# Softmax denominators: a running sum in a seventh plane of the exponentials' tile, added by VectorE instead of GpSimd

## The chip, the core and the metric

The kernel runs as one program on one core of a Trainium2 chip. The metric is the device time of the whole program in microseconds (us), the median of several executions. Five engines work beside each other and meet through semaphores: TensorE (PE; its weight loads are listed apart as PEld), VectorE (DVE), ScalarE (ACT), GpSimd (POOL), and SyncE (SP), which issues nearly all DMAs here.

## The reference

Two layers of a transformer-like step run over 2048 latent tokens ("sample") and 256 context tokens ("prompt"). Each layer normalises and modulates its input, projects it (1024 to 2816 columns), runs three branches (attention, a short convolution, a multi-scale pooling), gates each, and projects back. The change touches only the denominators of the attention:

```
s = jnp.einsum('bqkgd,btkd->bkgqt', qblk, k).astype(jnp.float32) * scale
p = jax.nn.softmax(s, axis=-1)
return jnp.einsum('bkgqt,btkd->bqkgd', p.astype(v.dtype), v)
```

There are 8 query heads over 2 key/value heads of width 64. A latent query attends to 2048 + 256 = 2304 keys; a context query to 256.

## The kernel before, in words

Each layer is a phase A (norm, projection, branches other than attention) and a phase B (attention and output projection). Everything is float32 in value; products are made of a rounded high part and a small low part, so that TensorE runs its fast formats.

Phase B is cut into units. A unit is one head and one block of 512 latent queries: 4 blocks x 8 heads = 32 units a layer, 64 in all. A unit has nine steps (`GRP = 3` of them form a group), and each step takes 256 keys. Besides, the first block of each layer holds four prompt units of one step each. The order of the work is written out by hand: one loop over all steps issues, in every step, a fixed set of pieces to each engine. Engines run their own queues strictly in that order.

In one step:

- `qk` (lines 1163 and 1164): four matmuls give the scores `st`, 128 keys x 2 x 512 queries, in PSUM. Two such tiles exist.
- `expo` (line 1173): ScalarE writes exp of them in full float32 to `P`, then (line 1175) once more in the rounded format to `ph`. GpSimd subtracts (`padd`, line 183) to get the low part `pl`.
- `pv` (line 1209, three steps later): two matmuls with `ph`; the low parts follow at a unit's end (line 1216).
- `max_pieces` (lines 1123 and 1130, on VectorE lines 1124 and 1132): two matmuls `mx` for a unit ahead, each followed by a row maximum `mr` on VectorE. Two `mx` tiles exist, so TensorE can issue the next but one only when VectorE has read its forerunner.
- pieces of the output projection (lines 1336 to 1340) for a block that is done.

The denominators are the sums of `P` over the keys. One part of that sum is over the 128 partitions, and is a small matmul with a column of constants (`fin_b`, line 1243, tile `lc`). The other is over the key tiles, within a partition: `zsum`. For each group of three steps the tile `P` holds, in each partition, 3 x 512 x 2 numbers: step, query, and the two key tiles of a step side by side. `expo` writes with a step of two elements (`"p n t -> p t n"`), so for one query the two key tiles are neighbours in memory. `zsum` sums the six numbers of each query with one `tensor_reduce` of VectorE over two axes, cut into three pieces of 152, 190 and 170 queries, one piece in each of the next three steps (list `zq`). It writes a tile `Z`. From the second group on, GpSimd adds the previous `Z` to it (two adds a unit), and that sum is what `lc` reads after the third.

The pools: `P` has 2 buffers, `Z` 3; the tail of the last block borrows the `Z` buffers for rows of the residual (`end`, `load_x(2, ...)`). `ch` is a tile of the output projection.

Of the kernel before, what the change touches and what calls it, by code (L numbers as in the profile page):

```python
# [9 lines left out]
F32 = mybir.dt.float32  # L10
# [4 lines left out]
ALU = mybir.AluOpType  # L15
AX = mybir.AxisListType
# [80 lines left out]
def hybrid_step(ctx: ExitStack, tc: tile.TileContext, A, O):  # L97
    nc = tc.nc
# [83 lines left out]
    def padd(out, a, b, op=ALU.add):  # L182
        nc.gpsimd.tensor_tensor(out=out, in0=a, in1=b, op=op)  # L183
# [820 lines left out]
    def phase_b(l, xs_src, xp_src, xs_dst, xp_dst, nxt):  # L1004
# [3 lines left out]
        with ExitStack() as st, ExitStack() as left:  # L1008
            def pool(name, bufs=1, side="right", to=st, **kw):
                return to.enter_context(tc.tile_pool(name=name, bufs=bufs, side=side, reuse_waits="tile", **kw))  # L1010
# [50 lines left out]
            def make_unit(prompt, blk, h):  # L1061
# [11 lines left out]
                u.fh = int(PR['fh'] and blk > 0)  # L1073
                u.P, u.pp, u.low, u.z = {}, {}, [], []
                return u
# [81 lines left out]
            GRP = 3  # L1157

            def qk(u, j):
# [4 lines left out]
                    nc.tensor.matmul(out=ps[:, i, :], lhsT=u.KL[u.g][0:65, kt], rhs=u.T2, start=False, stop=True)  # L1164
                return ps

            def expo(u, j, ps):
                if u.prompt:
                    u.P[0] = wk.tile([128, 1, 512, 2], F32, tag="wo", name="Pp", bufs=4)
                elif j % GRP == 0:  # L1170
                    u.P[j // GRP] = wk.tile([128, GRP, 512, 2], F32, tag="P", name="P", bufs=2)
                P = u.P[j // GRP][:, j % GRP].rearrange("p n t -> p t n")
                nc.scalar.activation(out=P, in_=ps, func=AF.Exp, scale=0.125)  # L1173
                ph = wk.tile([128, 2, 512], F32R, tag="ph", name="ph", bufs=LAG)
                nc.scalar.activation(out=ph, in_=ps, func=AF.Exp, scale=0.125)  # L1175
                pl = wk.tile([128, 2, 512], F16, tag="pl", name="pl", bufs=LAG + 8)
                if u is units[-1]:
                    for e, c in ((padd, slice(0, PR['dc'])), (dsub, slice(PR['dc'], 512))):
                        e(pl[:, 1, c], P[:, 1, c], ph[:, 1, c], ALU.subtract)
                    padd(pl[:, 0], P[:, 0], ph[:, 0], ALU.subtract)  # L1180
                else:
                    padd(pl, P, ph, ALU.subtract)
                u.pp[j] = (ph, pl)

            def zsum(u, grp, ns):

                st = {}
                cuts = [0, PR['z1'], PR['z2'], 512] if ns == GRP else [0, 512]

                def one(i):  # L1190
                    if i == 0:
                        st["z"] = wk.tile([128, 512], F32, tag="Z", name="Z", bufs=PR['zb'])
                    z = st["z"]
                    c = slice(cuts[i], cuts[i + 1])
                    nc.vector.tensor_reduce(out=z[:, c], in_=u.P[grp][:, 0:ns, c, :].rearrange("p s n t -> p n s t"),  # L1195
                                            axis=AX.XY, op=ALU.add)
                    if i == len(cuts) - 2:
                        if grp and (u.blk or grp == 1 or not PR['zl']):
                            padd(z, z, u.z.pop())
                        u.z.append(z)  # L1200

                return [lambda i=i: one(i) for i in range(len(cuts) - 1)]

# [186 lines left out]
            def outproj_tail(B):  # L1390
# [6 lines left out]
                def load_x(t, tag, n, bufs):  # L1397
                    xs[t] = []
                    for i in range(0, D, n):
                        x = wk.tile([128, n], F32, tag=tag, name="ox", bufs=bufs)  # L1400
                        nc.sync.dma_start(out=x, in_=xs_src[rows[t], i:i + n])
                        xs[t] += [x[:, k:k + 512] for k in range(0, n, 512)]
# [30 lines left out]
                    load_w(3, 0, wk.tile([128, KD, 256], F32R, tag="P", name="wt", bufs=2), 0)  # L1433

                def end():
                    load_x(2, "Z", 512, PR['zb'])
                    load_x(3, "o", 512, 2)

                def mm(t, c, q):
# [51 lines left out]
                for t in range(4):  # L1491
                    for c in range(4):
                        rest += [lambda t=t, c=c, q=q: mm(t, c, q) for q in ((2, 0, 1, 3) if 4 * t + c >= 4 + n2 else (3,))]
                        if c % 2:
                            rest.append(lambda t=t, c=c: add(t, c // 2))
                    rest.append(lambda t=t: finish(t))
                return early, half, later, final, end, ahead, rest, beside


# [95 lines left out]
            wk = pool("b_wk")  # L1595
# [9 lines left out]
            for s in range(NSTEP + LAG + 16):  # L1605
# [50 lines left out]
                if cur:  # L1656
                    u, j = cur
                    ps = qk(u, j)
                    if ready:
                        do_pv(s)  # L1660
                    expo(u, j, ps)
                    pvq.append((u, j, s))
                    if j % GRP == GRP - 1 or j == u.nst - 1:
                        zq.extend(zsum(u, j // GRP, j % GRP + 1))
# [19 lines left out]
            slow.flush()  # L1684

    phases = [phase_b(1, xS1, xP1, xS2, xP2, None)]
    phases.append(phase_a(1, xS1, xP1, phases[-1]))
    phases.append(phase_b(0, A["x_sample"][0], A["x_prompt"][0], xS1, xP1, phases[-1]))
    phases.append(phase_a(0, A["x_sample"][0], A["x_prompt"][0], phases[-1]))
    for phase in reversed(phases):  # L1690
# [30 lines left out]
```

## Time and profile before

| what | us |
|---|---|
| median of 3 runs | 3357.68 (3351.25 to 3362.43) |
| profiled execution, its own time | 3371.42 |
| its span in the profile | 3369.6 |
| phase B of the first layer, core stretch looked at | 721 to 1600 |
| phase B of the second layer, core stretch looked at | 2385 to 3300 |

The profiled execution is 13.7 us longer than the median of the runs. Busy times are those of one execution. A busy TensorE is not a TensorE at its peak, since the ends of its matmuls are modelled; so an idle TensorE in the rows is surely idle, while a busy one may be waiting within its pipeline. "Idle before" names what ended the wait of an engine.

### The profile page before, as it was taken

Reading aid. Unit: us, or ns where it says so; the run is one execution under the profiler, and the core shown is the slowest. Engines: PE = TensorE matmul, PEld = TensorE weight load, DVE = VectorE, ACT = ScalarE, POOL = GpSimd, SP = SyncE. Lnnn points to the kernel's source line nnn. Section 1 sums busy time; section 2 is a strip of 40 time slices with the busy share of each in tenths; the row PEclk is TensorE's granted clock in tenths of the full one; section 3 lists DMA queues with packets and bytes.
Section 4 is the critical chain, followed back from the end, with each engine's and each line's share of the span. In section 5 each row is a group of like instructions: output and inputs, shape, how many; then the busy total and the mean of one; then the engine's idle time right before and its main releaser. Section 6 shows DMA issues by size and latency. Waiting matters only on the chain. (4 is left out here: it accounts for less than half of the span.)

```text
span 3369.6 us, 48369 instructions
## 1 busy us (share of the span) xinstructions
PE 3138.9 (93%) x17818; PEld 2369.1 (70%) x17818; DVE 2446.6 (73%) x3860; ACT 1845.8 (55%) x2654; POOL 2125.9 (63%) x1192
## 2 busy tenths in 40 slices
PE   6899999988999999999999999999889899998998
PEld 4788888754566666667788787887456566665667
DVE  6546474458888888888466536635898988999885
ACT  3232333248777777777433323323787677776772
POOL 3325352238998898888453435322798888887883
PEclk9999999999999999999999999999899999999999
DMA  7246645350241323133523555334113324232245
GB/s 240 79 151 197 222 131 160 128 130 23 89 144 49 97 74 97 56 114 118 203 85 117 180 181 167 113 103 114 50 54 119 123 60 128 74 111 85 76 138 197
DMA packets 377380, 402.66 MB, mean 119 GB/s; under 512 B 21940, under 2 KB 329144, under 8 KB 376632
## 3 DMA queue, kind: packets, MB, share of 16 engines
q1 hardware_dynamic: 377144, 399.56, 38.3%
q8 instruction: 142, 2.33, 0.3%
q14 instruction: 94, 0.77, 0.1%
HBM read 278.09 MB, written 121.39 MB: 119 GB/s over the span
## 5 line engine op out<-in xcount | busy, mean ns | idle before, releaser
L183 POOL TENSOR_TENSOR pl<-P,ph 128x1024 f16<-128x1024 f32 (+2 forms) x594 | 1401.4, 2379 | 242.3 <-ACT ph L1175 223.2
L1124 DVE TENSOR_REDUCE mr<-mx 128x1 f32<-128x512 f32 x1024 | 693.9, 683 | 214.5 <-PE mx L1123 210.2
L1173 ACT ACTIVATE P<-st 128x1024 f32<-128x1024 f32 x576 | 635.1, 1103 | 324.9 <-PE st L1164 313.8
L1195 DVE TENSOR_REDUCE Z<-P 128x152 f32<-128x912 f32 (+2 forms) x576 | 695.4, 1208 | 13.5 <-ACT P L1173 12.6
L1175 ACT ACTIVATE ph<-st 128x1024 fp32r<-128x1024 f32 x584 | 592.2, 1014 | 0.0
L1123 PE MATMUL mx<-KH,T 128*128 128x512 f32 x1024 | 507.7, 496 | 56.8 <-DVE mr L1124 38.1
L1163 PE MATMUL st<-T,KH 128*128 128x512 f32 x1152 | 506.0, 498 | 9.6 <-ACT ph L1175 9.6
L638 PE MATMUL rest<-xh,wh 128*128 128x512 f32 (+1 forms) x1280 | 486.1, 380 | 1.9 <-ACT wh L428 1.5
L640 PE MATMUL rest<-xh,wl 128*128 128x512 f32 (+1 forms) x1280 | 476.7, 372 | 6.7 <-DVE wl L430 4.9
L639 PE MATMUL rest<-xl,wh 128*128 128x512 f32 (+1 forms) x1280 | 476.8, 372 | 0.8 <-POOL xl L183 0.8
L1164 PE MATMUL st<-T,L 65*128 65x512 f16 x1152 | 459.4, 399 | 0.0
L1209 PE MATMUL pv<-ph,V 128*128 128x512 f32 x1152 | 385.5, 416 | 11.5 <-DVE o L1228 11.5
L1164 PEld LDWEIGHTS <-L 65*128 65x128 f16 x1152 | 113.7, 99 | 302.7 <-issue 301.8
L1123 PEld LDWEIGHTS mx<-KH,T 128*128 128x128 f32 x1024 | 200.3, 196 | 169.7 <-DVE mr L1124 104.8
L430 POOL TENSOR_TENSOR wl<-wf,wh 128x512 fp32r<-128x512 f32 x88 | 121.9, 1386 | 300.5 <-ACT wh L428 285.1
L640 PEld LDWEIGHTS rest<-xh,wl 128*128 128x128 f32 x1280 | 244.1, 191 | 50.5 <-DVE wl L430 5.9
L638 PEld LDWEIGHTS rest<-xh,wh 128*128 128x128 f32 x1280 | 244.9, 191 | 47.2 <-issue 6.3
L639 PEld LDWEIGHTS rest<-xl,wh 128*128 128x128 f32 x1280 | 244.8, 191 | 38.5 <-POOL xl L183 1.2
L477 PE MATMUL qkv<-wh,xh 128*128 128x256 f32 x864 | 252.2, 292 | 3.1 <-ACT wh L428 3.1
L478 PE MATMUL qkv<-wl,xh 128*128 128x256 f32 x864 | 248.8, 288 | 5.3 <-DVE wl L430 2.8
L1163 PEld LDWEIGHTS st<-T,KH 128*128 128x128 f32 x1152 | 229.8, 200 | 26.4 <-ACT ph L1175 12.7
L479 PE MATMUL qkv<-wh,xl 128*128 128x256 f32 x864 | 247.9, 287 | 0.0
(231 smaller groups left out, 5833.0 us busy)
## 6 DMA issues: line engine op xcount, KB each, us to landing
wo<-woH SPq DMA_DIRECT2D x68, 512.0 KB
wo<-woL SPq DMA_DIRECT2D x68, 512.0 KB
wf<-in_w_in SPq DMA_DIRECT2D x50, 512.0 KB
wa<-in_w_ada SPq DMA_DIRECT2D x24, 1024.0 KB
wf<-in_w_in SPq DMA_DIRECT2D x19, 1024.0 KB
woH<-wgh SPq DMA_DIRECT2D x64, 256.0 KB
woL<-wgl SPq DMA_DIRECT2D x64, 256.0 KB
xS<-ox SPq DMA_DIRECT2D x24, 512.0 KB
```

The lines of the kernel that those rows point to most:

```text
L183: nc.gpsimd.tensor_tensor(out=out, in0=a, in1=b, op=op)
L638: nc.tensor.matmul(out=ps[:, 0:b.n], lhsT=wh[:, k, ms], rhs=b.h[:, k, :], start=(k == 0), stop=False)
L639: nc.tensor.matmul(out=ps[:, 0:b.n], lhsT=wh[:, k, ms], rhs=b.l[:, k, :], start=False, stop=False)
L640: nc.tensor.matmul(out=ps[:, 0:b.n], lhsT=wl[:, k, ms], rhs=b.h[:, k, :], start=False, stop=(k == KD - 1))
L1123: nc.tensor.matmul(out=ps, lhsT=u.T1[:, q * 128:(q + 1) * 128], rhs=u.KH[u.g][:, c * 512:(c + 1) * 512])
L1124: nc.vector.reduce_max(out=mr[:, q, c:c + 1], in_=ps, axis=AX.X)
L1163: nc.tensor.matmul(out=ps[:, i, :], lhsT=u.KH[u.g][:, kt], rhs=u.T1, start=True, stop=False)
L1164: nc.tensor.matmul(out=ps[:, i, :], lhsT=u.KL[u.g][0:65, kt], rhs=u.T2, start=False, stop=True)
L1173: nc.scalar.activation(out=P, in_=ps, func=AF.Exp, scale=0.125)
L1175: nc.scalar.activation(out=ph, in_=ps, func=AF.Exp, scale=0.125)
L1195: nc.vector.tensor_reduce(out=z[:, c], in_=u.P[grp][:, 0:ns, c, :].rearrange("p s n t -> p n s t"), axis=AX.XY, op=ALU.add)
L1209: nc.tensor.matmul(out=u.po, lhsT=u.V[u.g][:, 2 * j + i, :], rhs=ph[:, i, :], start=(j == 0 and i == 0), stop=False)
```

## The change

`P` becomes a tile of seven planes of 512 numbers each. The six planes of a group's exponentials lie one behind the other (key tile by key tile, each contiguous), so `expo` writes, and `pl` reads, contiguously. The seventh plane (index `2 * GRP`) holds the running sum of the earlier groups: `zsum` of a group writes its result into the seventh plane of the *next* group's tile (which `new_planes` allocates at that moment), and that next group's `tensor_reduce` reads seven planes instead of six. Only the third group writes to `Z`, of which one buffer is left. GpSimd's adds go. The reduction is now over one axis: for each query it takes six or seven numbers, each 512 elements (2048 bytes) behind the one before. Prompt units write their denominators into a tile that borrows the tag `ch`; the tail borrows `zs` where it borrowed `Z`.

```
-                elif j % GRP == 0:
-                    u.P[j // GRP] = wk.tile([128, GRP, 512, 2], F32, tag="P", name="P", bufs=2)
-                P = u.P[j // GRP][:, j % GRP].rearrange("p n t -> p t n")
+                elif j == 0:
+                    new_planes(u, 0)
+                P = u.P[j // GRP][:, 2 * (j % GRP):2 * (j % GRP) + 2]
...
+                u.P[grp] = wk.tile([128, 2 * GRP + 1, 512], F32, tag="P", name="P", bufs=2)
...
                     if i == 0:
-                        st["z"] = wk.tile([128, 512], F32, tag="Z", name="Z", bufs=PR['zb'])
+                        if not u.prompt and grp < 2:
+                            new_planes(u, grp + 1)
+                            st["z"] = u.P[grp + 1][:, 2 * GRP]
+                        elif u.prompt:
+                            if not u.h:
+                                zps.append(wk.tile([128, 4, 512], F32, tag="ch", name="Zp", bufs=1))
+                            st["z"] = zps[0][:, u.pair]
+                        else:
+                            st["z"] = wk.tile([128, 512], F32, tag="Z", name="Z", bufs=1)
...
-                    nc.vector.tensor_reduce(out=z[:, c], in_=u.P[grp][:, 0:ns, c, :].rearrange("p s n t -> p n s t"),
-                                            axis=AX.XY, op=ALU.add)
-                    if i == len(cuts) - 2:
-                        if grp and (u.blk or grp == 1 or not PR['zl']):
-                            padd(z, z, u.z.pop())
-                        u.z.append(z)
+                    nc.vector.tensor_reduce(
+                        out=st["z"][:, c], in_=u.P[grp][:, 0:2 * ns + (1 if grp else 0), c].rearrange("p s n -> p n s"),
+                        axis=AX.X, op=ALU.add)
...
-                    load_x(2, "Z", 512, PR['zb'])
+                    load_x(2, "zs", 512, 2)
```

VectorE's queue in the first layer's first block, around the end of one group and the beginning of the next. `mr` and `m` are maxima, `o` the attention output, and the number behind a name tells one tile from another. Before:

```order
L1195 TENSOR_REDUCE Z_7944<-P_7853 128x170
L1124 TENSOR_REDUCE mr_8001<-mx_8016 128x1
L1267 TENSOR_TENSOR o_7913<-o_7913,rlb_8020 128x256
L1140 TENSOR_REDUCE m_8024<-mr_7742 128x4
L1124 TENSOR_REDUCE mr_8001<-mx_8033 128x1
L1195 TENSOR_REDUCE Z_8036<-P_7951 128x152
L1124 TENSOR_REDUCE mr_8001<-mx_8049 128x1
L1267 TENSOR_TENSOR o_7588<-o_7588,rlb_8052 128x512
L1124 TENSOR_REDUCE mr_8001<-mx_8061 128x1
L1195 TENSOR_REDUCE Z_8036<-P_7951 128x190
```

The same place after the change:

```order
L1210 TENSOR_REDUCE P_7925<-P_7836 128x170
L1124 TENSOR_REDUCE mr_7981<-mx_7996 128x1
L1279 TENSOR_TENSOR o_7895<-o_7895,rlb_8000 128x256
L1140 TENSOR_REDUCE m_8004<-mr_7727 128x4
L1124 TENSOR_REDUCE mr_7981<-mx_8013 128x1
L1210 TENSOR_REDUCE P_8016<-P_7925 128x152
L1124 TENSOR_REDUCE mr_7981<-mx_8028 128x1
L1279 TENSOR_TENSOR o_7576<-o_7576,rlb_8031 128x512
L1124 TENSOR_REDUCE mr_7981<-mx_8040 128x1
L1210 TENSOR_REDUCE P_8016<-P_7925 128x190
```

No place in the queue moved. The pieces write into the next group's `P`, and the first piece of the second group reads the tile that the last piece of the first group wrote.

GpSimd's queue over two units (one pair of heads) of a later block, from one gating multiply `o` to the next. Before:

```order
L183 TENSOR_TENSOR o<-o,zs 128x512
L183 TENSOR_TENSOR Z<-Z 128x512
L183 TENSOR_TENSOR pl<-P,ph 128x1024 x3
L183 TENSOR_TENSOR Z<-Z 128x512
L183 TENSOR_TENSOR pl<-P,ph 128x1024 x6
L183 TENSOR_TENSOR Z<-Z 128x512
L183 TENSOR_TENSOR pl<-P,ph 128x1024 x3
L183 TENSOR_TENSOR Z<-Z 128x512
L183 TENSOR_TENSOR pl<-P,ph 128x1024 x6
L183 TENSOR_TENSOR o<-o,zs 128x512
```

After, over three such pairs:

```order
L183 TENSOR_TENSOR pl<-P,ph 128x1024 x18
L183 TENSOR_TENSOR o<-o,zs 128x512
L183 TENSOR_TENSOR pl<-P,ph 128x1024 x18
L183 TENSOR_TENSOR o<-o,zs 128x512
L183 TENSOR_TENSOR pl<-P,ph 128x1024 x18
```

The four adds of a pair are gone; the 18 subtractions of a pair follow each other.

## Rows read from the trace of the kernel before

**Rows 1.** Page, span and engines: busy us (share of the span), instructions.
```profile
span 3369.6 us, 48369 instructions
...
PE 3138.9 (93%) x17818; PEld 2369.1 (70%) x17818; DVE 2446.6 (73%) x3860; ACT 1845.8 (55%) x2654; POOL 2125.9 (63%) x1192
```

**Rows 2.** Stretches: us, busy us by engine (instructions), PE clock, DMA share, GB/s.
```profile
721.00:1600.00 879.00, 833.99 (x4533) 558.80 (x4532) 756.60 (x1021) 658.77 (x825) 768.95 (x356) 0.98 0.30 88
2385.00:3300.00 915.00, 853.51 (x4579) 571.39 (x4578) 816.92 (x1090) 673.90 (x924) 766.96 (x361) 0.97 0.31 93
2611.40:2695.70 84.30, 75.07 (x396) 48.57 (x396) 81.69 (x104) 56.35 (x75) 68.16 (x33) 0.98 0.39 124
```

**Rows 3.** Groups by line: shapes, count, busy us, mean ns, idle before and releasers.
```profile
L183 POOL TENSOR_TENSOR pl<-P,ph 128x1024 f16<-128x1024 f32 (+2 forms) x594 | 1401.4, 2379 | 242.3 <-ACT ph L1175 223.2 <-PE mx L1123 13.6 <-PE pv L1209 1.7
L1195 DVE TENSOR_REDUCE Z<-P 128x152 f32<-128x912 f32 (+2 forms) x576 | 695.4, 1208 | 13.5 <-ACT P L1173 12.6
L1124 DVE TENSOR_REDUCE mr<-mx 128x1 f32<-128x512 f32 x1024 | 693.9, 683 | 214.5 <-PE mx L1123 210.2
L1173 ACT ACTIVATE P<-st 128x1024 f32<-128x1024 f32 x576 | 635.1, 1103 | 324.9 <-PE st L1164 313.8 <-DVE Z L1195 6.4
L1175 ACT ACTIVATE ph<-st 128x1024 fp32r<-128x1024 f32 x584 | 592.2, 1014 | 0.0
...
L183 POOL TENSOR_TENSOR Z<-Z 128x512 f32<-128x512 f32 x128 | 166.7, 1303 | 99.9 <-DVE Z L1195 86.4 <-PE st L1164 7.2 <-PE pv L1216 2.5
...
L1279 DVE TENSOR_TENSOR mixl<-o,mixh 128x512 fp32r<-128x512 f32 (+1 forms) x40 | 77.8, 1946 | 3.4 <-ACT mixh L1274 3.4
...
L430 DVE TENSOR_TENSOR wl<-wf,wh 128x512 fp32r<-128x512 f32 x88 | 76.6, 872 | 155.8 <-ACT wh L428 154.1 <-DMA qH<-qh 1.2
```

**Rows 4.** VectorE in order of time: start, duration us, instruction, [idle before].
```profile
1100.30 1.21 DVE L1195 TENSOR_REDUCE Z<-P 128x170 f32<-128x1020 f32 x1
...
1102.86 1.09 DVE L1195 TENSOR_REDUCE Z<-P 128x152 f32<-128x912 f32 x1
...
1104.47 2.97 DVE L1279 TENSOR_TENSOR mixl<-o,mixh 128x512 fp32r<-128x512 f32 x1
1107.37 0.41 DVE L1340 TENSOR_TENSOR ox<-ox,op 128x256 f32<-128x256 f32 x1
...
1108.30 1.33 DVE L1195 TENSOR_REDUCE Z<-P 128x190 f32<-128x1140 f32 x1
...
1113.35 0.69 DVE L1124 TENSOR_REDUCE mr<-mx 128x1 f32<-128x512 f32 x1 [3.13 <-PE mx L1123]
```

**Rows 5.** Instructions on the prompt units' exponentials: count, ns min/median/max, first and last start.
```profile
L1195 DVE TENSOR_REDUCE Z<-Pp x8: 1219/1220/1222, 761.4 to 2479.8; 128x512 f32<-128x1024 f32 x8
```

**Rows 6.** Waits, 721 to 1600: total us, times, longest us.
```profile
ACT P L1173 <- PE st L1164: 154.9, 174, 5.3
...
DVE mr L1124 <- PE mx L1123: 107.6, 143, 3.8
...
POOL Z L183 <- DVE Z L1195: 34.4, 25, 3.8
...
PE mx L1123 <- DVE mr L1124: 9.4, 16, 1.2
...
PEld lc L1243 <- POOL pl L183: 2.1, 8, 0.4
```

**Rows 7.** TensorE in order of time, around the stall at 1107.
```profile
1105.35 0.59 PE L1123 MATMUL mx<-KH,T 128*128 128x512 f32 x1
1107.83 0.40 PE L1336 MATMUL op<-wo,ch 128*128 128x256 f32 x1 [1.89 <-DVE ox L1340]
```

**Rows 8.** Stretches around that stall, columns as in rows 2.
```profile
1105.00:1108.00 3.00, 1.11 (x6) 0.43 (x5) 3.00 (x3) 2.72 (x3) 3.00 (x2) 1.00 0.00 0
1108.00:1110.00 2.00, 2.00 (x8) 1.43 (x8) 2.00 (x3) 0.00 (x0) 2.00 (x2) 0.52 0.66 213
```

More of the change, by code (lines that the diff above doesn't have):

```diff
@@ L1165, in qk, with new_planes @@
                 return ps
+            def new_planes(u, grp):
+                u.P[grp] = wk.tile([128, 2 * GRP + 1, 512], F32, tag="P", name="P", bufs=2)
             def expo(u, j, ps):
                 if u.prompt:
-                    u.P[0] = wk.tile([128, 1, 512, 2], F32, tag="wo", name="Pp", bufs=4)
-                elif j % GRP == 0:
-                    u.P[j // GRP] = wk.tile([128, GRP, 512, 2], F32, tag="P", name="P", bufs=2)
-                P = u.P[j // GRP][:, j % GRP].rearrange("p n t -> p t n")
+                    u.P[0] = wk.tile([128, 2, 512], F32, tag="wo", name="Pp", bufs=4)
+                elif j == 0:
+                    new_planes(u, 0)
+                P = u.P[j // GRP][:, 2 * (j % GRP):2 * (j % GRP) + 2]
                 nc.scalar.activation(out=P, in_=ps, func=AF.Exp, scale=0.125)
@@ L1183, in expo @@
                 u.pp[j] = (ph, pl)
+            zps = []
             def zsum(u, grp, ns):
@@ L1191, in one @@
                     if i == 0:
-                        st["z"] = wk.tile([128, 512], F32, tag="Z", name="Z", bufs=PR['zb'])
-                    z = st["z"]
-                    c = slice(cuts[i], cuts[i + 1])
-                    nc.vector.tensor_reduce(out=z[:, c], in_=u.P[grp][:, 0:ns, c, :].rearrange("p s n t -> p n s t"),
-                                            axis=AX.XY, op=ALU.add)
-                    if i == len(cuts) - 2:
-                        if grp and (u.blk or grp == 1 or not PR['zl']):
-                            padd(z, z, u.z.pop())
-                        u.z.append(z)
+                        if not u.prompt and grp < 2:
[7 more added lines that the diff above has]
+                            st["z"] = wk.tile([128, 512], F32, tag="Z", name="Z", bufs=1)
+                    if i == len(cuts) - 2 and (u.prompt or grp == 2):
+                        u.z.append(st["z"])
+                    c = slice(cuts[i], cuts[i + 1])
+                    nc.vector.tensor_reduce(
+                        out=st["z"][:, c], in_=u.P[grp][:, 0:2 * ns + (1 if grp else 0), c].rearrange("p s n -> p n s"),
+                        axis=AX.X, op=ALU.add)
                 return [lambda i=i: one(i) for i in range(len(cuts) - 1)]
```

## The prediction

> **What bounds the kernel now.** I read the page's engine line first: TensorE is busy for 93% of the span, VectorE 73%, GpSimd 63% [rows 1]. These are means over two unlike phases, so I read next the stretches of attention, where alone the change works [rows 2]. There the picture is tighter. The two stretches last 879.0 and 915.0 us, 1794.0 together. TensorE is busy 1687.5 of them (94%), VectorE 1573.5 (88%), GpSimd 1535.9 (86%). So VectorE's whole idle time in attention is 220.5 us; that is the cover any new work on VectorE has.
>
> Third, who waits for whom, and last [rows 6]: VectorE's idle time is nearly all waiting for a score matmul (`mr` <- `mx`, 107.6 us in the first layer), while TensorE waits only 9.4 us for the reverse. So TensorE sets the pace now and VectorE follows close behind. GpSimd's adds of `Z` wait for VectorE (34.4 us in the first layer, 86.4 in all [rows 3, 6]), but hardly anyone waits for them: the denominators' weight loads waited 2.1 us for GpSimd. The step is one VectorE queue with two `mr` of 683 ns and one piece of the sum of 1208 ns [rows 3]; a stretch with more VectorE work runs it at 81.69 of 84.30 us, 97%, with TensorE down to 89% [rows 2]. That is how the kernel looks when VectorE is the bound.
>
> **The change, part by part.**
>
> *GpSimd loses 128 adds* of 1303 ns, 166.7 us of work and 86.4 us of waiting [rows 3]. What remains on GpSimd is `pl`, which is needed at a unit's end. Nothing on the path ended with it, so I count the removal itself at nothing. Its side effect: VectorE's subtraction `mixl` takes 1946 ns on average where the like-shaped `wl` takes 872 [rows 3], and the one of 2.97 us in the rows made TensorE wait 1.89 us [rows 4, 7]. These are two-input instructions of VectorE beside a busy GpSimd. The excess is 40 x 1.07 = 43 us. GpSimd's share falls from 86% to under 60% in what follows, by about a third: -14 us of VectorE (bounds 0 and -43).
>
> *ScalarE writes `P` contiguously.* It took 1103 ns with the step of two and the contiguous `ph` takes 1014 [rows 3]. At best 576 x 0.09 = 51 us of ScalarE go; it waits 154.9 us for scores in the first layer alone [rows 6], so: nothing.
>
> *VectorE sums seven planes in two groups of three.* Before, a unit sums 3 x 3072 = 9216 elements a partition, after it 3072 + 2 x 3584 = 10240. The three sizes of piece (912, 1020, 1140 elements) took 1.09, 1.21, 1.33 us [rows 4], which is 1.05 ns an element and 0.13 us fixed; 576 pieces of 1208 ns agree (1024 elements on average). At that price the added 1024 elements x 64 units cost 69 us, less than the idle 220.5.
>
> *VectorE now reads every element from another place.* This is the term that decides, and no row of before shows it. Before, the reduction took two neighbouring elements, then jumped; and such a pair cost 2 x 1.05 = 2.1 ns, the same per element as with no jump at all (`mr`, 512 contiguous elements in 683 ns [rows 3]). So a visit to one place costs at most 2.1 ns, and a pair fills it. After, each visit yields one element. The bounds: 1.05 ns an element, if a visit is free, and 2.1, if a visit lasts that long whatever it yields. Only one neighbouring row speaks on strides: ScalarE's `P`, written with a step of two elements, took 9% longer than the contiguous `ph` from the same input [rows 3], so distance in memory is not free. I take the upper end, 2.1, because a single element per visit leaves nothing that could hide the visit, and keep 1.05 for the range.
>
> [...]
>
> The sum at 2.1: 10240 x 2.106 = 21.57 us and 9 x 0.13 = 1.17 us fixed, 22.74 us a unit, x 64 = 1455 us against 695.4 [rows 3]: +760. The eight prompt pieces (1024 elements, 1.22 us [rows 5]) gain 1.08 us each: +9. Together +769.
>
> *New waits.* The first piece of a group now writes into the next group's `P`, so it waits until GpSimd has read that buffer's last content, four steps earlier; behind it in the queue stand the maxima, for which TensorE waits. Before, ScalarE's write to the same buffer had the same wait a few hundred ns later, and it never was the last one (ScalarE waited for scores [rows 6]). Nothing. Within VectorE the next piece reads what an earlier one wrote, with one or more maxima between: nothing. The borrowed `ch` and `zs` are free by then: nothing, at most a few us in each tail if a load comes later.
>
> *The sum.* VectorE's work in attention becomes 1573.5 + 769 - 14 = 2328 us, more than TensorE's 1687.5, and more than the 1794 that the stretches last. VectorE becomes the bound; at the 97% of the stretch where it already is [rows 2], attention takes 2328 / 0.969 = 2403 us, 609 more than now. The rest is unchanged. The profiled execution, 3371.4 us, becomes 3980; its runs' median lies 13.7 lower: 3966. Ends of this case: no idle time and the whole 43 us saved, 2299 us of attention, 3863; VectorE idle for 8%, 2328 / 0.92 = 2530 us, 4094.
>
> **The rivals.**
>
> *TensorE falls to its lower clock (B).* If TensorE waits in every step, its clock may fall. [...] For it: TensorE would be busy for 70% of a VectorE-bound stage. Against it: at 89% busy the clock was 0.98 [rows 2]. TensorE's work of 1687.5 at 0.975 is 1645 at full clock, 3290 at half. If a tenth of the stage's work runs at that level, the stage takes 0.9 x 2403 + 0.1 x 3290 = 2492 and the program 4055; at a third, 4263.
>
> *A smaller price for the visit (C).* If the truth lies in the middle, 1.58 ns, the 655 thousand elements (10240 x 64) cost VectorE 69 + 655 x 0.527 and the prompts 4, 418 us more in all, the stage takes (1573.5 + 418 - 14) / 0.969 = 2041 us: 3604. For it: ScalarE's stride cost 9%, not 100%. Against it: a pair hid its visit without a trace.
>
> *Full pace, VectorE late (D2).* The visit is free, and the 69 us come on the path in full, since VectorE stands at 88% and feeds TensorE's `mx` buffers: 3427.
>
> *Full pace, all hidden (D1), the other side.* The 69 us disappear in the 220.5 us that VectorE waits for `mx`, and GpSimd's lighter load spares some of the `mixl` stalls that TensorE sees (one cost 1.89 us and a slow clock after it): 3350, no slower than before. It decides as long as an element costs less than 1.05 + (220.5 - 69) / 655 = 1.28 ns; above that VectorE has no cover left.
>
> That the change does not do what it says can't be: the adds are gone from GpSimd's queue and the seventh plane is read.
>
> **How the numbers follow.** The forecast (A) 0.72, B 0.07, C 0.07, D2 0.06, D1 0.08. The forecast's own range is 3863 to 4094. The range of all runs from 3450, which takes in C, to 4110, which takes in A and the lower part of B: about 0.70 + 0.03 + 0.07. A measurement of this kernel tells 0.3% (10 us) from no change, since its three runs spread by that much. A, B, C and D2 are slower by more; of D1, 3 in 100 are faster by more and 5 within.
>
> **What would show it.** Right: the pieces of the sum at 2.0 to 2.9 us where they were 1.1 to 1.3; VectorE over 95% busy in attention, TensorE waiting for `mr` in nearly every step, GpSimd without `Z` and under 60% busy; each attention phase about 300 us longer, the projection phases unchanged. Wrong: six-plane pieces still at 1.1 to 1.3 us, which is D at once. If the pieces are slow but the time is over 4110, look at the granted clock.

## The result, and the profile after

The kernel became slower: 3769.33 us (3766.08 to 3772.8) against 3355.03 us, a ratio of 1.1227, 95% interval 1.1204 to 1.1251. That is 414 us more; the prediction had 609 more. The profiled execution spans 3764.1 us, 394.5 more than before.

Busy time by engine on the page of the kernel after:

```profile
span 3764.1 us, 48129 instructions
...
PE 3309.7 (88%) x17818; PEld 2427.3 (64%) x17818; DVE 2974.2 (79%) x3860; ACT 1817.9 (48%) x2654; POOL 1933.9 (51%) x1064
```

Against [rows 1], VectorE gained 528 us, more than the span did; GpSimd lost 192. The stretches of attention, with columns as in [rows 2]:

```profile
721.00:1811.00 1090.00, 935.19 (x4667) 595.01 (x4665) 1025.81 (x1039) 664.09 (x848) 701.87 (x308) 0.94 0.24 72
2585.00:3700.00 1115.00, 932.55 (x4559) 599.01 (x4559) 1062.58 (x1082) 658.09 (x915) 674.26 (x303) 0.92 0.26 78
```

VectorE is now busy for 94% and 95% of them, where it was 86% and 89%; GpSimd for 62%. These stretches are parts of attention, and not the same work as in [rows 2]; attention as a whole is measured behind the experiments. The granted clock of TensorE fell from 0.98 and 0.97 to 0.94 and 0.92.

The groups of instructions that answer to [rows 3] (the two VectorE groups with `P` as input are the pieces of the sum):

```profile
L183 POOL TENSOR_TENSOR pl<-P,ph 128x1024 f16<-128x1024 f32 (+2 forms) x594 | 1367.2, 2306 | 916.7 <-ACT ph L1179 852.3 <-PE mx L1123 18.2 <-issue 17.9
L1210 DVE TENSOR_REDUCE P<-P 128x152 f32<-128x912 f32 (+5 forms) x384 | 815.9, 2125 | 7.0 <-ACT P L1177 6.9
...
L1177 ACT ACTIVATE P<-st 128x1024 f32<-128x1024 f32 x576 | 589.5, 1023 | 626.8 <-PE st L1164 552.5 <-DVE Z L1210 63.9 <-DVE P L1210 4.9
...
L1123 PE MATMUL mx<-KH,T 128*128 128x512 f32 x1024 | 531.8, 520 | 261.7 <-DVE mr L1124 228.8 <-DVE mr L1132 23.6 <-ACT T L1153 2.3
...
L1210 DVE TENSOR_REDUCE Z<-P 128x152 f32<-128x1064 f32 (+2 forms) x192 | 435.6, 2271 | 2.1 <-ACT P L1177 1.1
...
L1291 DVE TENSOR_TENSOR mixl<-o,mixh 128x512 fp32r<-128x512 f32 (+1 forms) x40 | 57.4, 1435 | 2.7 <-ACT mixh L1286 2.7
```

The pieces cost 815.9 + 435.6 = 1251.5 us, 556 more than the 695.4 of before, in the same 576 instructions. TensorE's `mx` matmuls waited 38.1 us for `mr` over the whole run before; now 228.8. The row of before:

```profile
L1123 PE MATMUL mx<-KH,T 128*128 128x512 f32 x1024 | 507.7, 496 | 56.8 <-DVE mr L1124 38.1 <-ACT T L1153 10.1 <-DVE mr L1132 2.4
```

Single pieces, VectorE in order of time:

```profile
1207.02 1.99 DVE L1210 TENSOR_REDUCE P<-P 128x170 f32<-128x1020 f32 x1
...
1210.20 2.08 DVE L1210 TENSOR_REDUCE P<-P 128x152 f32<-128x1064 f32 x1
...
1213.41 2.51 DVE L1210 TENSOR_REDUCE P<-P 128x190 f32<-128x1330 f32 x1
```

The first reads six planes of 170 queries, as many elements as the 1.21 us piece of [rows 4]; it takes 1.99 us. The other two read seven. From 152 to 190 queries of seven planes, 266 elements, 0.43 us are added: 1.6 ns an element, where it was 1.05. But the prompt pieces, two planes of 512 queries, hardly changed, 1248 against 1220 ns in [rows 5]:

```profile
L1210 DVE TENSOR_REDUCE Zp<-Pp x8: 1243/1248/1256, 764.0 to 2682.1; 128x512 f32<-128x1024 f32 x8
```

That row contradicts a price for each visit, and the first experiment follows it up.

### The profile page after: what moved, and what is told of

The parts are those of the page before. It is cut to its first block, busy times and chain, and to the rows that moved or that the text cites. A ratio compares the mean times of both kernels' runs of the same rounds, so it can differ in the third digit from the quotient of the medians.

```text
span 3764.1 us, 48129 instructions
## 1 busy us (share of the span) xinstructions
PE 3309.7 (88%) x17818; PEld 2427.3 (64%) x17818; DVE 2974.2 (79%) x3860; ACT 1817.9 (48%) x2654; POOL 1933.9 (51%) x1064
## 5 line engine op out<-in xcount | busy, mean ns | idle before, releaser
L183 POOL TENSOR_TENSOR pl<-P,ph 128x1024 f16<-128x1024 f32 (+2 forms) x594 | 1367.2, 2306 | 916.7 <-ACT ph L1179 852.3
L1177 ACT ACTIVATE P<-st 128x1024 f32<-128x1024 f32 x576 | 589.5, 1023 | 626.8 <-PE st L1164 552.5
L1210 DVE TENSOR_REDUCE P<-P 128x152 f32<-128x912 f32 (+5 forms) x384 | 815.9, 2125 | 7.0 <-ACT P L1177 6.9
L1123 PE MATMUL mx<-KH,T 128*128 128x512 f32 x1024 | 531.8, 520 | 261.7 <-DVE mr L1124 228.8
L1163 PE MATMUL st<-T,KH 128*128 128x512 f32 x1152 | 536.2, 524 | 9.8 <-ACT ph L1179 9.8
L1123 PEld LDWEIGHTS mx<-KH,T 128*128 128x128 f32 x1024 | 209.4, 205 | 445.0 <-DVE mr L1124 357.0
L1164 PE MATMUL st<-T,L 65*128 65x512 f16 x1152 | 482.6, 419 | 0.0
L1210 DVE TENSOR_REDUCE Z<-P 128x152 f32<-128x1064 f32 (+2 forms) x192 | 435.6, 2271 | 2.1 <-ACT P L1177 1.1
L1221 PE MATMUL pv<-ph,V 128*128 128x512 f32 x1152 | 405.4, 435 | 11.6 <-DVE o L1240 7.8
L1163 PEld LDWEIGHTS st<-T,KH 128*128 128x128 f32 x1152 | 243.5, 211 | 25.2 <-ACT ph L1179 12.6
```

The costliest lines, as they stand in the source:

```text
L1123: nc.tensor.matmul(out=ps, lhsT=u.T1[:, q * 128:(q + 1) * 128], rhs=u.KH[u.g][:, c * 512:(c + 1) * 512])
L1163: nc.tensor.matmul(out=ps[:, i, :], lhsT=u.KH[u.g][:, kt], rhs=u.T1, start=True, stop=False)
L1210: nc.vector.tensor_reduce(out=st["z"][:, c], in_=u.P[grp][:, 0:2 * ns + (1 if grp else 0), c].rearrange("p s n -> p n s"), axis=AX.X, op=A ...
L1221: nc.tensor.matmul(out=u.po, lhsT=u.V[u.g][:, 2 * j + i, :], rhs=ph[:, i, :], start=(j == 0 and i == 0), stop=False)
```

## The experiments

**Reading alone (p1_forms).** A kernel of its own: VectorE sums one tile in many shapes, nothing else runs. The lines that matter, `s` planes at distance `d` elements:

```
L48 to L55  512 queries, s = 1 to 8, d = 512
L56, L57    170 queries, s = 6, d = 513, 514
L60, L65    170 queries, s = 6, d = 528, 256
L67         170 queries, s = 6, d = 1024
L69         170 queries, s = 6, d = 512
L70         120 queries, 16 bytes from one to the next, s = 2, d = 512
L73 to L76  160 queries, s = 6, a step of 4, 8, 12, 16 bytes within the query
L79, L80    170 queries, 3 and 4 pairs (the layout before)
```

> This kernel computes nothing of the reference: it runs sums of VectorE over one tile, alone, in many shapes, three times each, to price the read by itself. After the change a piece of six planes took 1.78, 1.98, 2.17 us (152, 170, 190 queries), so 1.7 ns an element, but the prompt pieces, two planes, 1.25 us against 1.22, so no price at all. Theory 1 (few places are kept): neighbouring queries lie in the same small line, and VectorE keeps a few such lines; up to some number of planes between 2 and 6 a visit is free, above it each visit costs 1.7 ns, at any distance. Expects: 170 queries of six planes about 1.98 us at distances of 513 to 1028 elements as at 512; two planes with queries 16 bytes apart (no line shared) slow, 120 x 2 elements at 1.7 ns or more (0.5 us or more, against 0.38); a sharp step between 2 and 6 planes. Theory 2 (the distance of 2048 bytes): planes at a power of two collide in the same part of the memory. Expects: six planes at 516, 520 or 528 elements at the pace of pairs (about 1.2 us), 256 and 1024 slow. Theory 3 (a price for each query, whatever the distance): expects a time that grows with the number of queries and not with the place, so six contiguous numbers slow as well. Pairs (3 x 2) should take 1.2 us in all three.

Measured (groups by line, columns as in [rows 3]):

```profile
L55 DVE TENSOR_REDUCE o<-x 128x512 f32<-128x4096 f32 x3 | 21.1, 7031 | 0.1
L54 DVE TENSOR_REDUCE o<-x 128x512 f32<-128x3584 f32 x3 | 18.5, 6178 | 0.1
L53 DVE TENSOR_REDUCE o<-x 128x512 f32<-128x3072 f32 x3 | 16.0, 5325 | 0.1
...
L51 DVE TENSOR_REDUCE o<-x 128x512 f32<-128x2048 f32 x3 | 11.0, 3655 | 0.1
...
L57 DVE TENSOR_REDUCE o<-x 128x170 f32<-128x1020 f32 x3 | 6.0, 2011 | 0.1
...
L56 DVE TENSOR_REDUCE o<-x 128x170 f32<-128x1020 f32 x3 | 5.8, 1919 | 0.1
L50 DVE TENSOR_REDUCE o<-x 128x512 f32<-128x1536 f32 x3 | 5.7, 1913 | 0.1
...
L67 DVE TENSOR_REDUCE o<-x 128x170 f32<-128x1020 f32 x3 | 5.6, 1871 | 0.1
...
L65 DVE TENSOR_REDUCE o<-x 128x170 f32<-128x1020 f32 x3 | 5.6, 1870 | 0.1
...
L69 DVE TENSOR_REDUCE o<-x 128x170 f32<-128x1020 f32 x3 | 5.6, 1869 | 0.1
L60 DVE TENSOR_REDUCE o<-x 128x170 f32<-128x1020 f32 x3 | 5.6, 1868 | 0.1
...
L76 DVE TENSOR_REDUCE o<-x 128x160 f32<-128x960 f32 x3 | 5.5, 1833 | 0.1
L80 DVE TENSOR_REDUCE o<-x 128x170 f32<-128x1360 f32 x3 | 4.7, 1570 | 0.1
L75 DVE TENSOR_REDUCE o<-x 128x160 f32<-128x960 f32 x3 | 4.2, 1414 | 0.1
...
L49 DVE TENSOR_REDUCE o<-x 128x512 f32<-128x1024 f32 x3 | 3.7, 1235 | 0.1
L79 DVE TENSOR_REDUCE o<-x 128x170 f32<-128x1020 f32 x3 | 3.6, 1216 | 0.1
...
L73 DVE TENSOR_REDUCE o<-x 128x160 f32<-128x960 f32 x3 | 3.5, 1153 | 0.1
L74 DVE TENSOR_REDUCE o<-x 128x160 f32<-128x960 f32 x3 | 3.5, 1153 | 0.1
...
L70 DVE TENSOR_REDUCE o<-x 128x120 f32<-128x240 f32 x3 | 1.8, 603 | 0.1
```

Read the 512-query rows upwards. Two and three planes take 1235 and 1913 ns; the fourth adds 1742 ns, and each one from there about 850. Taking 0.13 us of each as fixed, up to three planes an element costs 1.1 to 1.2 ns, from four on 1.7. The distance does not help: 256, 512, 528 and 1024 elements all take 1.87 us, and the distances that are no multiple of 16 elements take 3 to 8% more (513 and 514: 1.92 and 2.01 us), so theory 2 falls. Six contiguous numbers go at full pace (1153), and so do six at 8 bytes; at 12 bytes they are a quarter slower (1414), at 16 bytes slow (1833). So theory 3, which expected contiguous numbers to be slow, falls too. When neighbouring queries lie 16 bytes apart, even two planes are slow: (603 - 130) / 240 = 2.0 ns an element. Four pairs are as cheap per element as three (1570 against 1216 ns). What theory 1 forecast came out: a sharp step, between three and four planes (1913 and 3655 ns), slow reads of six at every distance shown (1.87 to 2.01 us), and slow reads at two planes already when neighbouring queries lie 16 bytes apart. Its picture, that VectorE keeps a few small lines at hand, is not shown, only the effect.

**The layout alone (e1_six_planes).** Six planes, GpSimd's adds as before:

```
-                    u.P[0] = wk.tile([128, 1, 512, 2], F32, tag="wo", name="Pp", bufs=4)
+                    u.P[0] = wk.tile([128, 2, 512], F32, tag="wo", name="Pp", bufs=4)
...
-                    u.P[j // GRP] = wk.tile([128, GRP, 512, 2], F32, tag="P", name="P", bufs=2)
-                P = u.P[j // GRP][:, j % GRP].rearrange("p n t -> p t n")
+                    u.P[j // GRP] = wk.tile([128, 2 * GRP, 512], F32, tag="P", name="P", bufs=2)
+                P = u.P[j // GRP][:, 2 * (j % GRP):2 * (j % GRP) + 2]
...
-                    nc.vector.tensor_reduce(out=z[:, c], in_=u.P[grp][:, 0:ns, c, :].rearrange("p s n t -> p n s t"),
-                                            axis=AX.XY, op=ALU.add)
+                    nc.vector.tensor_reduce(out=z[:, c], in_=u.P[grp][:, 0:2 * ns, c].rearrange("p s n -> p n s"),
+                                            axis=AX.X, op=ALU.add)
```

> The layout alone: six contiguous planes, reduced over one axis, while GpSimd adds two Z a unit as before. Theory (the read's price, 1.7 ns an element from more than three places, measured alone in p1): pieces of 1.78, 1.98, 2.17 us, VectorE 64 x 17.8 = 1137 us for them against 695, so 442 more in attention; at 95% busy, (1573.5 + 442) / 0.95 = 2122 us of attention against 1794, and the program at about 3680 (3650 to 3700). Rival (the layout is harmless, the seventh plane or its waits cost): 3355 within 1%.

Measured: 3685.01 us, ratio 1.0977 (1.0958 to 1.0996).

```profile
L1195 DVE TENSOR_REDUCE Z<-P 128x152 f32<-128x912 f32 (+2 forms) x576 | 1140.2, 1980 | 9.8 <-ACT P L1173 8.8
```

VectorE's pieces cost 445 us more than before, with the same elements, and the program 326. The theory's 3650 to 3700 holds and the rival (a harmless layout) falls. The layout is four fifths of the loss. What the kernel after adds to it, the seventh plane on VectorE with GpSimd's adds gone, is the other 84 us (3769 - 3685), for 111 us more in the pieces.

**GpSimd's adds taken away (e2_no_adds).** The denominators hold only the last group's sum:

```
-                            padd(z, z, u.z.pop())
+                            u.z.pop()
```

> The kernel before without GpSimd's two adds a unit; the denominators are those of the last group alone. It prices what the change could save on GpSimd. Theory (GpSimd ends nothing on the path): 3355 within 0.3%. Rival (GpSimd's load slows VectorE's two-input subtractions and so TensorE): up to 43 us less, 3312 to 3345, with mixl well under 1946 ns.

Measured: 3342.34 us, ratio 0.9957 (0.9942 to 0.9972). So the adds were worth about 14 us, 0.4%: that bounds what moving them elsewhere could gain in the kernel before. VectorE's busy time fell by 32 us, and `mixl` is 16 of them, from 1946 to 1550 ns:

```profile
L1279 DVE TENSOR_TENSOR mixl<-o,mixh 128x512 fp32r<-128x512 f32 (+1 forms) x40 | 62.0, 1550 | 3.2 <-ACT mixh L1274 3.2
```

The time lies in the rival's range, near its upper end; the theory (nothing, within 0.3%) is missed narrowly. But the rival's cause is not shown. `mixl` was as short with GpSimd's adds in place (e1_six_planes, the first row) and as long as before without them (e5_three_planes below, the second):

```profile
L1279 DVE TENSOR_TENSOR mixl<-o,mixh 128x512 fp32r<-128x512 f32 (+1 forms) x40 | 57.5, 1437 | 2.7 <-ACT mixh L1274 2.7
L1291 DVE TENSOR_TENSOR mixl<-o,mixh 128x512 fp32r<-128x512 f32 (+1 forms) x40 | 78.4, 1960 | 11.0 <-ACT mixh L1286 10.5
```

So its length does not follow from whether GpSimd adds; what it does follow stays open.

**The adds on VectorE, pairs kept (e3_adds_on_vector).**

```
-                            padd(z, z, u.z.pop())
+                            dsub(z, z, u.z.pop(), ALU.add)
```

(`dsub` is VectorE's two-input instruction.)

> The adds moved to VectorE as two tensor_tensor of 512 elements a unit, with pairs as before: the move without the layout. VectorE gets 128 adds of 0.7 to 1.9 us (two inputs beside a busy GpSimd), 90 to 240 us more in attention against 220 idle. Theory (VectorE has cover for little): 3360 to 3450. Rival (any new work on VectorE comes on the path in full, and this is what made the change slow): 3355 + 240 and more.

Measured: 3463.84 us, ratio 1.0316 (1.03 to 1.0333), just above the theory's range and far from the rival's.

```profile
L186 DVE TENSOR_TENSOR Z<-Z 128x512 f32<-128x512 f32 x128 | 139.9, 1093 | 4.4
```

VectorE's busy time grew by 99 us (139.9 for the adds, less what shorter `mixl` and others gave back), and the program by 105. Over the whole of attention VectorE was idle for 248 us before and for 246 here: it used none of it. So the rival's mechanism holds here, new work on the path in full, though not its price for the adds. Each add stands in VectorE's queue right behind a piece of the sum and ahead of the next `mr`; a version with the adds at another place was not run, so this shows no cover for work at that place, and not for work anywhere.

**Four planes (e4_four_planes) and three (e5_three_planes).** The kernel after, each piece reading only its last planes:

```
-                        out=st["z"][:, c], in_=u.P[grp][:, 0:2 * ns + (1 if grp else 0), c].rearrange("p s n -> p n s"),
+                        out=st["z"][:, c], in_=u.P[grp][:, 2 * ns + (1 if grp else 0) - 4 if ns == GRP else 0:2 * ns + (1 if grp else 0), c].rearrange("p s n -> p n s"),
```

(`- 3` in the second. Neither sums the whole of the denominators.)

> The kernel after, but each piece reads four of its planes (the last four, the running sum among them); the rest of the sum is left out. It has the change's layout, waits and missing adds, and fewer elements than before (four a query, not six). Theory (price of a place): four planes cost 6.8 ns a query as p1 measured, so pieces of 1.16, 1.29, 1.42 us, near to the six in pairs (1.09, 1.21, 1.33), and the time is near to that of the kernel before: 3335 to 3380. Rival 1 (planes are read at 1.05 ns an element and something else of the change costs, its waits or the shared tile): pieces of 0.77 to 0.93 us, time over 3450. Rival 2 (each read from a plane costs 2.1 ns): pieces of 1.4 to 1.73 us, over 3400.

> As e4_four_planes, but each piece reads three planes (the last three); the rest of the sum is left out. p1 measured 3.5 ns a query for three planes, read at nearly 1.1 ns an element, where four cost 6.8. Theory (a few places are kept, up to three; and VectorE's work is on the path though it is only 88% busy, as e3_adds_on_vector suggests, where 106 us more of VectorE made 105 us more of time): pieces of 0.7 to 0.95 us, so a plane less takes some 0.45 us off each piece, 260 us off VectorE against e4, and the time falls below the kernel before, to 3200 to 3300. Rival 1 (TensorE sets the pace as soon as VectorE is under about 88%): 3325 to 3350. Rival 2 (the price is one for each place read, with no step between three and four): pieces of 1.0 to 1.2 us.

Measured: four planes 3382.0 us, ratio 1.0069 (1.0052 to 1.0087); three planes 3276.85 us, ratio 0.976 (0.9732 to 0.9788). The pieces of the third group, with four planes and with three:

```profile
L1210 DVE TENSOR_REDUCE Z<-P x192: 1168/1372/1558, 748.4 to 3318.4; 128x152 f32<-128x608 f32 x64, 128x190 f32<-128x760 f32 x64, 128x170 f32<-128x680 f32 x64
```

```profile
L1210 DVE TENSOR_REDUCE Z<-P x192: 659/736/811, 748.5 to 3216.1; 128x152 f32<-128x456 f32 x64, 128x190 f32<-128x570 f32 x64, 128x170 f32<-128x510 f32 x64
```

A plane less, a quarter of the elements, nearly halves the piece: 1372 to 736 ns. The step between three and four is there in the kernel too, and four elements read this way cost more than six in pairs (a median of 1204 before). Both runs have the shared tile, its waits, the contiguous writes and the missing adds, and neither is far from the kernel before; so none of these is the loss. e5's theory holds (3200 to 3300); where it speaks of 106 us more of VectorE in e3_adds_on_vector, the page has 99. The rivals of the two runs fall (2.1 ns an element would have made the four-plane pieces 1.4 us at least; they begin at 1.17); the four-plane time is 2 us above the theory's range, and its pieces came out at 1.37 us where 1.29 was expected.

**A version faster than both (e6_mixl_on_gpsimd).** The kernel before, with `mixl` on GpSimd instead of VectorE, where it took 1946 ns:

```
-nc.vector.tensor_tensor(out=lo[:, 0:n], in0=o[:, 0:n], in1=h[:, 0:n], op=ALU.subtract)
+padd(lo[:, 0:n], o[:, 0:n], h[:, 0:n], ALU.subtract)
```

> The kernel before with the 40 subtractions mixl on GpSimd instead of VectorE. They took 1946 ns on VectorE beside a busy GpSimd, and one of 2.97 us held up TensorE for 1.9 us. VectorE loses 78 us, GpSimd gains 40 x 1.2 = 48. Theory (VectorE's work in attention is on the path nearly in full): 60 to 80 us of the two layers go, 3280 to 3300. Rival (TensorE sets the pace and VectorE's idle time is cover): 3340 to 3360.

Measured: 3330.23 us, ratio 0.9918 (0.9892 to 0.9944): faster than both kernels, but only by 28 us or 0.8%, between the theory's 60 to 80 and the rival's nothing; neither range holds it. The 40 instructions take 1188 ns on GpSimd:

```profile
L183 POOL TENSOR_TENSOR mixl<-o,mixh 128x512 fp32r<-128x512 f32 (+1 forms) x40 | 47.5, 1188 | 1.5 <-ACT mixh L1274 1.5
```

All runs together. Attention is taken here from the start of a layer's first exponential to the start of its last piece of the sum; VectorE's idle time in it is its length less VectorE's busy time. For the kernel before and the kernel after, both layers (columns as in [rows 2]):

```profile
721.30:1642.80 921.50, 869.42 (x4738) 583.42 (x4736) 784.78 (x1057) 689.17 (x860) 807.24 (x383) 0.98 0.30 89
2338.60:3308.90 970.30, 894.13 (x4738) 594.34 (x4736) 859.30 (x1145) 712.78 (x973) 811.21 (x383) 0.97 0.32 97
```

```profile
721.70:1835.30 1113.60, 952.73 (x4754) 607.31 (x4754) 1045.98 (x1057) 675.04 (x861) 714.89 (x320) 0.94 0.25 75
2523.10:3709.00 1185.90, 990.34 (x4772) 632.81 (x4771) 1123.48 (x1145) 699.72 (x974) 714.46 (x320) 0.91 0.27 80
```

| kernel | VectorE busy, whole run, us | VectorE idle in attention, us | time, us |
|---|---|---|---|
| e5_three_planes | 2190.6 | 409 | 3277 |
| e6_mixl_on_gpsimd | 2367.6 | 283 | 3330 |
| e2_no_adds | 2414.9 | 263 | 3342 |
| before | 2446.6 | 248 | 3358 |
| e4_four_planes | 2489.4 | 218 | 3382 |
| e3_adds_on_vector | 2545.4 | 246 | 3464 |
| e1_six_planes | 2873.8 | 144 | 3685 |
| after | 2974.2 | 130 | 3769 |

So attention grew by 408 us: VectorE's work in it by 525, its idle time shrank by 118. Below the kernel before, a microsecond of VectorE is worth a third to a half of one (256 us less in e5 gave 81, 79 in e6 gave 28, 32 in e2 gave 16). Above it there is no single price: about half in e4 (43 us more cost 23), 1.1 in e3, nearly 0.8 in e1 and in the kernel after (528 us cost 414). That reads as a kernel in which TensorE and VectorE take turns in setting the pace; what makes e3 dearer than e4 was not tested.

## Why the prediction was right, and where its size was off

*The deciding term.* Right in kind: VectorE's reads from separate places became dear, VectorE became the bound, TensorE waited for `mr`. Wrong in its picture: a visit that costs the same "whatever it yields" would have made every piece slow, but the prompt pieces, with two visits a query, gained 0.03 us each and not 1.08, and p1_forms reads three planes at nearly full pace; the price begins with the fourth place. And off in size: the step "I take the upper end, 2.1, because a single element per visit leaves nothing that could hide the visit". Measured, an element costs 1.7 ns alone (p1_forms) and 1.8 in the kernel after, with 0.13 us of each piece as fixed. The term came to 556 us, not 769. With it in the prediction's own sum: (1573.5 + 556 - 14) / 0.969 = 2183 us of attention, and 3371.4 + 389 - 13.7 = 3747; measured 3769. The likeliest case's own range, from 3863, was missed. The time lies between it and case C's 3604, and the wide range held it only because it reached over both; C's 1.58 ns was the nearer price.

*The bounds from the rows held.* That a visit costs at most the 2.1 ns that a pair took gave the upper end, and 1.7 to 1.8 lies inside. Numbers 8 bytes apart cost no more than contiguous ones in p1_forms (1153 ns both), those 16 bytes apart 1833 ns; and taking another place each time costs little while two or three planes alternate (1.1 to 1.2 ns an element). The lower bound, full pace, falls: 1.99 us for a piece that took 1.21.

*The removal of GpSimd's adds* was counted at 14 us less of VectorE's work through `mixl`, with bounds of 0 and 43. In e2_no_adds VectorE's work shrank by 32 us, 16 of them `mixl`, and the program by 14: that the two figures of 14 agree is luck, since one is VectorE's work and the other time. In the kernel after, `mixl` saved 40 x 0.51 = 20 us, as much as in e1_six_planes, which kept the adds.

*Idle time as cover.* The sum let 97% of the stage fill with VectorE's work; it is 94.7% (2088 of 2205 us). With that share the sum gives 3798 instead of 3747, 29 us too many instead of 22 too few; it is no finer than that. The premise that all of VectorE's idle time is cover is wrong: of 248 us in attention the change used 118, e3_adds_on_vector none. D1, which hid 69 us of work there, was not tested at full pace. By the dearest and the cheapest addition measured (99 us of work for 105 of time in e3; 75 for 40 from e2 to e4, both without GpSimd's adds), 69 us would have cost 37 to 73, an estimate; D2 had the better reasoning. A sign was there before: the prediction counted 9.4 us for which matmuls `mx` waited for `mr` in the first layer, but their weight loads had waited another 36.9 in the same stretch.

*ScalarE's write and the new waits*, both counted at nothing: `P` fell to 1023 ns and ScalarE waited longer for scores (552.5 us before `P` over the run, 313.8 before). The first piece's new wait for GpSimd does not show among the releasers of the pieces (7.0 and 2.1 us of idle in all, nearly all for ScalarE). A wait that I had not listed appeared: ScalarE's `P` waited 63.9 us for late pieces to free the buffer (6.4 before). Nothing shows it on the path.

*TensorE's clock (B).* It fell, to 0.94 and 0.92 in the stretches above. By the trace's record of the clock TensorE was granted 0.5 of its full clock in 341 us of attention, against 98 before, and 1.0 in the rest, and about a tenth of the matmuls of attention began in these 341 us. So B's condition, a tenth of the stage's work at that level, was met; the half in B's sum is that level, which [rows 8] show as a granted 0.52 over 2 us. B's price for it, 89 us more than A (2492 against 2403 us), was not paid: in these 341 us VectorE was busy for 311, 91%. It was idle in them for 30 us, and for 26 us in the 98 us of before. B let a stage that VectorE fills take TensorE's time. How much of VectorE's other 100 us of idle time comes after such a stretch stays open.

*The signs named in advance.* Pieces at 2.0 to 2.9 us: 1.72 to 2.57. VectorE over 95% busy: 94 and 95. TensorE waiting for `mr` in nearly every step: 239 of the 1024 matmuls `mx` waited, and 337 of their weight loads. GpSimd without `Z` and under 60%: 62. Each attention phase about 300 us longer: 192 and 216, by the size of the term. The projection phases unchanged: what lies outside attention was 13 us shorter.

## What to carry to other kernels

Before a tile is laid out anew, look at what the reader of it gets per place: a sum over separate planes went at nearly the pace of pairs up to three (1.1 to 1.2 ns an element against 1.05), and cost 1.6 to 1.7 times as much an element from four on (1.7 to 1.8), though the program had the same pieces and only a ninth more elements. Two sums of three planes in place of one of six, which these numbers invite, were not run. Price a move between engines on the engine that receives it, by its worth there: GpSimd's 167 us were worth 14, the 528 new ones of VectorE 0.8 each. Here the idle time of an engine at 88% beside a neighbour at 94% was no sure cover: one addition hid about half of itself, another nothing. Test that with a small addition, at the place in the queue where the work will stand, before counting on it.

## What the runs showed of the hardware

- VectorE's sum over planes costs 1.1 to 1.2 ns an element for up to three planes 2 KB apart, 1.7 for four to eight (p1_forms; 1.8 in the kernel after); six planes of 170 queries take 1.87 us at distances of 1, 2 and 4 KB alike. Within a query, six numbers of 160 queries take 1153 ns at steps of 4 and 8 bytes, 1414 at 12, 1833 at 16 and 1867 at 32 (p1_forms).
- ScalarE's write slows down between steps of 8 and 16 bytes too, from 669 to 1129 ns: 512 elements at steps of 4, 8, 16 and 32 bytes, in this order from the bottom (p1_forms):

```profile
L90 ACT ACTIVATE y<-x 128x512 f32<-128x512 f32 x3 | 3.4, 1135 | 0.1
L89 ACT ACTIVATE y<-x 128x512 f32<-128x512 f32 x3 | 3.4, 1129 | 0.1
L88 ACT ACTIVATE y<-x 128x512 f32<-128x512 f32 x3 | 2.0, 669 | 0.1
L87 ACT ACTIVATE y<-x 128x512 f32<-128x512 f32 x3 | 1.9, 629 | 11.8 <-DVE y L45 11.7
```

- The same 40 two-input subtractions `mixl` took on average 1946 ns on VectorE in the kernel before, 1148 to 1960 in the other runs, long and short ones with and without GpSimd's adds, and 1188 on GpSimd itself.
- On TensorE a product of rounded numbers is one matmul here, one of full float32 two: 864 for the 864 products of `qkv` (line 477), 283 ns each, and 384 for the 192 of `aps` (line 232), 379 ns each (128x256, medians, kernel before).
